# Gate and up of an encoder layer: a second block product by quarter blocks, both in four chained parts

## The chip, the cores and the metric

The kernel runs on one core of a Trainium2 chip. The metric is the device time of one execution in microseconds (us); lower is better. Five engines run side by side, each through its own queue in order: PE (TensorE, matrix products into the accumulator banks), DVE (VectorE), ACT (ScalarE), POOL (GpSimd) and SP, which here only issues transfers. They wait for each other through semaphores.

## The reference

One layer of a bidirectional encoder on 1024 tokens of width 1024, in float32. All but its feed-forward part is left out here:

```
mix = concat(retention, windowed attention) @ w_out
h   = layer_norm(ALPHA * x + mix)                       # (1024, 1024)
g   = h @ w_ffn_gate;   up = h @ w_ffn_up               # (1024, 2816) each
ffn = (silu(g) * up) @ w_ffn_down                       # (1024, 1024)
out = layer_norm(ALPHA * h + ffn + sigmoid(h @ w_pg) * (p @ w_pe))
```

## The kernel before

Each float32 operand is held as two parts, a high part in a shorter format and the remainder (`split`: ScalarE copies the high part, L71, then VectorE subtracts it, L72). A product of two such operands is three matmuls (`mm3c`, L783 to L785).

The large products are done by a scheme with seven block products in place of eight. In gate and up the 22 tiles of 128 hidden units are taken in 11 pairs (`Pair`, n = 0 to 10). The left matrix of a pair, once for gate (m = 0) and once for up (m = 1), is 2 by 2 blocks of 128 hidden units by 512 of the width; the right matrix is the transposed h, 2 by 2 blocks of 512 by 512 in `HB` and, for the sums of blocks that the scheme needs, `TT`. `RIGHT[p]` is the right operand of product p, p = 1 to 7. A *unit* is one product for gate or up: `mm`, 12 matmuls of 512 columns. A bank W takes products 1, 6, 7 and 4 one after another; between them ScalarE copies the running sum to s1, u2, u3. Products 5 and 3 share a bank Z, product 2 has X. The output blocks are c11 = s1 + product 2, c22 = u3 + Z after 5, c21 = W after 4, c12 = u2 + Z after 3; then comes silu(gate) * up (`finish`), and from these sums for the down product (`asum`), stored in `ad`. Left operands are prepared ahead (`prep`: sums of blocks on VectorE, then `split`) into eight operand slots; `raw` and `ln` hold the loaded weights.

From pair 2 on (`FROM`), product 2 is itself done by the seven-product scheme, one level down: quarter blocks of 256 by 256 right columns, for gate and up together (they are the two block rows). That makes 42 matmuls of 256 columns where there were 24 of 512. They come in three parts (`FINE`), with a unit of product 6 between them. Their four right operands that are sums are formed once by VectorE (`fine_right`), each behind a given unit of pairs 0 and 1, in one buffer of 512 columns: three (or two) sums and a split. `prep_fine` prepares the left sums, `post_fine` adds the results to c11 piece by piece.

The order on every engine is written by the recording loop at the end: for each unit k its matmuls, its post, then a piece of `fine`, then preparations of later units (`ahead_g`) as long as slots are free, they lie at most nine units ahead, and the planner's costs fit into the next unit's time: 0.62 for a split, 1.24 for two sums, and so on, less the post's cost and `debt`, which a piece of `fine` raises by 2.2. Stores are issued a given number of units later. Then the down stage (lines from L1410 on) multiplies by w_ffn_down with operands loaded from `ad`.

Of the kernel before, what the change touches and what calls it, by code (L numbers as in the profile page):

```python
# [16 lines left out]
P = 128  # L17
# [25 lines left out]
def layer(tc, xT, xn, w_first, w_mt, w_rv, w_out, w_pg, w_pe, pT, w_gu, w_dn,  # L43
# [1117 lines left out]
    sarena = arena8  # L1161
# [3 lines left out]
    FINE = ((1, 6, 5), (7, 2), (4, 3))  # L1165
    FROM = 2
    evs, nev = [], [0]
    oslots = []
    fright, fsum = {}, []

    def pair_tile():
        nev[0] += 1
        return evs[(nev[0] - 1) % len(evs)]
# [7 lines left out]
    def fine_right(R):  # L1181

        x = cst[:, 0:HF].rearrange("p (k c) -> p k c", k=2)

        def blk(i, j, part):
            return R[:, part, 2 * i:2 * i + 2, j * Q:(j + 1) * Q]

        def both(left, right):
            dve.tensor_tensor(x, blk(*left, 0).bitcast(F32), blk(*right, 0).bitcast(F32), ALU.subtract)
            dve.tensor_tensor(x, x, blk(*left, 1).bitcast(F32), ALU.add)  # L1190
            dve.tensor_tensor(x, x, blk(*right, 1).bitcast(F32), ALU.subtract)

        def less(left):
            dve.tensor_tensor(x, blk(*left, 0).bitcast(F32), x, ALU.subtract)
            dve.tensor_tensor(x, x, blk(*left, 1).bitcast(F32), ALU.add)

        for q, (i, j) in {1: (0, 0), 2: (1, 0), 3: (1, 1)}.items():
            fright[q] = blk(i, j, 0), blk(i, j, 1)
        other = a_tile([P, 2, 2, Q], "fine", dt=F32R)
        fright[7] = other[:, 0], other[:, 1]  # L1200
        fright[5] = tuple(ct([P, 2, Q], "sg", 2, F32R) for _ in range(2))
        fright[6] = tuple(ct([P, 2, Q], "p", 2, F32R) for _ in range(2))
        fright[4] = blk(0, 1, 0), blk(0, 1, 1)
        return [lambda: (both((1, 1), (0, 1)), split(x, *fright[7])), lambda: (both((0, 1), (0, 0)), split(x, *fright[5])),
                lambda: (less((1, 1)), split(x, *fright[6])), lambda: (less((1, 0)), split(x, *fright[4]))]
# [3 lines left out]
    class Pair:  # L1209


        def __init__(self, n):
            self.n = n
            self.raw, self.ops, self.bank, self.ev, self.s, self.fine = {}, {}, {}, {}, {}, {}
# [8 lines left out]
        def sums(self, p, m):  # L1223
            a = lambda i, j: self.raw[m, i, j]
            s = self.s.setdefault(m, [sarena[:, 4 * m + k, :] for k in range(4)])
            if p == 6:
                dve.tensor_tensor(s[1], a(1, 0), a(1, 1), ALU.add)
                dve.tensor_tensor(s[0], s[1], a(0, 0), ALU.subtract)  # L1228
            else:
                dve.tensor_tensor(s[2], a(0, 0), a(1, 0), ALU.subtract)  # L1230
                dve.tensor_tensor(s[3], a(0, 1), s[0], ALU.subtract)
# [9 lines left out]
        def prep_fine(self, part):  # L1241

            f = self.fine

            def xy():
                return [self.raw[m, 0, 1] for m in range(2)]
# [24 lines left out]
            return [[(0, 1.1, sums), (1, 0.62, whole), (1, 0.36, lambda: put(6, fsum[1])), (1, 0.36, lambda: put(5, fsum[0]))],  # L1271
                    [(0, 0.36, lambda: put(7, fsum[2], 5))], [(1, 1.1, last)]][part]

        def mm_fine(self, part):

            if part == 0:
                self.fb = [bank(ptags[(3 * self.n + 1) % 4]) for _ in range(2)]
            for q in FINE[part]:
                t, c0 = self.fine[q]
                i, j = {1: (0, 0), 2: (0, 0), 6: (0, 1), 7: (0, 1), 5: (1, 0), 3: (1, 0), 4: (1, 1)}[q]  # L1280
                o = self.fb[i][:, j * Q:(j + 1) * Q]
                hi, lo = fright[q]
# [3 lines left out]
            for q in ((6,), (7, 2), (4,))[part]:  # L1286
                free_op(self.fine[q][0])

        def post_fine(self, part):

            ev = self.ev
            if part == 0:
                ev["c11"] = pair_tile()
            o, v = ev["c11"], ev["s1"]
            (c11, c12), (c21, c22) = ([o[:, m, j * Q:(j + 1) * Q] for j in range(2)] for m in range(2))
            (bx, by), (bz, bw) = ([b[:, j * Q:(j + 1) * Q] for j in range(2)] for b in self.fb)
            low = o[:, 1, :].rearrange("p (j c) -> p j c", j=2)

            def add(out_, x, y):
                dve.tensor_tensor(out_, x, y, ALU.add)  # L1300

            def twice(b):
                return b.unsqueeze(1).to_broadcast([P, 2, Q])

            if part == 0:
                add(c12, v[:, 0, Q:], bx)
                add(low, v[:, 1, :].rearrange("p (j c) -> p j c", j=2), twice(bx))
                add(c12, c12, by)
            elif part == 1:
                add(low, low, twice(by))  # L1310
                add(c22, c22, bz)
                add(c11, v[:, 0, :Q], bx)
            else:
                add(c12, c12, bz)
                add(c21, c21, bw)
                self.finish("c11", 0)
                self.finish("c11", 1)

        def mm(self, p, m):
            g = {1: 0, 6: 0, 7: 0, 4: 0, 2: 1, 5: 2, 3: 2}[p]  # L1320
            first = p in (1, 2, 5)
            if first:
                self.bank[g, m] = bank(ptags[(3 * self.n + g + (2 if g == 1 and self.n == 0 else 0)) % 4])
# [17 lines left out]

        def post(self, p, m, k):
            ev, W, X, Z = self.ev, self.bank.get((0, m)), self.bank.get((1, m)), self.bank.get((2, m))

            def get(name, over=None):
                if m == 0:
                    ev[name] = ev[over] if over else pair_tile()
                return ev[name][:, m, :]

            def add(name, left, right, over=None):  # L1350
                dve.tensor_tensor(get(name, over), ev[left][:, m, :], right, ALU.add)  # L1351
# [3 lines left out]
            wait = 2 if self.n < NP - 1 else 8  # L1355
            if p == 1:
                act.activation(get("s1"), W, AF.Copy)
# [5 lines left out]
            elif p == 7:  # L1363
                act.activation(get("u3"), W, AF.Copy)
                add("c22", "u3", Z, "u3")
                self.finish("c22", m)
            elif p == 4:
                c = get("c21", "s1")
                if m == 0:
                    act.activation(c, W, AF.Silu)  # L1370
                else:
                    dve.tensor_tensor(c, s("c21"), W, ALU.mult)
                    self.asum("c21", a("c21"), a("c11"), ALU.subtract)
                    stores.append((k + wait, lambda: sp.dma_start(ad[self.n, 2, :, 0, :], s("c21"))))
                    self.asum("c11", s("c21"), a("c22"), ALU.subtract)
                    stores.append((k + wait, lambda: sp.dma_start(ad[self.n, 0], ev["c11"])))
                    self.asum("c22", a("c22"), a("c21"), ALU.subtract)
                    stores.append((k + wait, lambda: sp.dma_start(ad[self.n, 3], ev["c22"])))
            elif p == 3:
                add("c12", "u2", Z, "u2")  # L1380
                self.finish("c12", m)
                if m:
                    self.asum("c12", a("c12"), s("c11"), ALU.add)
                    stores.append((k + wait, lambda: sp.dma_start(ad[self.n, 1], ev["c12"])))
# [5 lines left out]
    def g_unit(n, p, m, k):  # L1390
        pr = pairs2[n]

        def sums():
            pr.sums(p, m)
            if n + 1 < NP and p == 5:
                pairs2[n + 1].load(m, (0,))
# [7 lines left out]
        if p == 6:  # L1404
            items.insert(0, (0, 1.24, sums))
        elif p == 5:
            items.append((0, 1.24, sums))
        after = {2: (0.62, 1.24), 7: (0.62, 1.24), 4: (0, 2.5), 3: (0.62, 1.9)}.get(p, (0, 0))[m]
        return items, lambda: pr.mm(p, m), lambda: pr.post(p, m, k), 2.72, after

    def f_unit(n, part):
        pr = pairs2[n]
        return pr.prep_fine(part), lambda: pr.mm_fine(part), lambda: pr.post_fine(part), (2.16, 1.44, 1.44)[part], 1.45

    for n in range(NP):
        for p in (1, 6, 5, 7, 4, 3) if n >= FROM else (1, 2, 6, 5, 7, 4, 3):
            for m in range(2):
                if n >= FROM and p == 6:
                    gunits.append(f_unit(n, m))
                gunits.append(g_unit(n, p, m, len(gunits)))  # L1420
            if n >= FROM and p == 6:
                gunits.append(f_unit(n, 2))
# [331 lines left out]
    with tc.manual_schedule(engines={ET.PE, ET.DVE, ET.Activation, ET.Pool, ET.SP}):  # L1754
# [3 lines left out]
        fine = fine_right(RIGHT[2])  # L1758
        evs.extend(a_tile([P, 2, HF], "ev") for _ in range(7))
        fsum.extend([cst[:, 0:Q], cst[:, Q:2 * Q], cst[:, 2 * Q:3 * Q], ct([P, Q], "fs", 1)])  # L1760
        ahead_g(-1, 4)
        for k in range(NG):
            gunits[k][1]()
            gunits[k][2]()
            if k in (8, 11, 16, 19):
                fine.pop(0)()
                debt[0] += 2.2
# [4 lines left out]
            if j == -6:  # L1772
                arenas_a()
                op_arena(ct([P, 4, 2, HF], "h0a", dt=F32R))
                op_arena(big16((P, 4, 2, HF)))
                op_arena(big16((P, 4, 2, HF)))
                arena("chain", ct([P, 8, HF], "h0b"), 8)
            if j == -4:
                op_arena(big16((P, 4, 2, HF)))
                arena("b", big.tile([P, 8, HF], F32, tag="H", bufs=4, name=nm("H")), 8)  # L1780
            if j >= -6:
                ahead(0, j + 7)
            if j >= -4:
                ahead(1, j + 5)
        arena("chain", ct([P, 8, HF], "h2"), 8)
# [89 lines left out]
```

## Time and profile before

| | |
|---|---|
| median of 3 runs | 1176.09 us (1175.69 to 1176.13) |
| profiled execution | 1176.84 us, span 1175.1 us |
| granted TensorE clock | 0.998 |
| busy: PE, DVE, ACT, POOL | 1164.5, 845.1, 565.1, 119.2 us |
| gate and up | from 540.8 to 956.6 us of the span |
| down stage | from 956.6 us |

A row of the trace gives the start in us, the duration, engine, line and operation, output <- input by the program's names (buffer numbers left out), shapes, a count where equal rows were merged, and in brackets the engine's idle time before it and what released it. The duration of a row is longer than the distance to the next one where rows overlap in the engine.

### The profile page before, as it was taken

To read this page: it belongs to the slowest core of one execution; us is meant where nothing else is said; L and a number is where in the kernel's file an instruction comes from. 1 tells how busy PE (TensorE), PEld (TensorE's weight loads), DVE (VectorE), ACT (ScalarE), POOL (GpSimd) and SP (SyncE) were. 2 spreads that over 40 slices of the span, in tenths; PEclk is the share of its full clock that TensorE was granted. 3 is DMA by queue.
4 is the path that set the end of the run, shared out by engine and by line. 5 is a ranking of instruction groups with operands and counts; after the bars stand their busy time and mean duration, and the time that the engine had idled before them with its cause. 6 is when DMAs were issued, how large, how long until landed. Compare 5 with 4: busy or idle time off the path is not lost.

```text
span 1175.1 us, 17378 instructions
## 1 busy us (share of the span) xinstructions
PE 1164.5 (99%) x6230; PEld 973.8 (83%) x6230; DVE 845.1 (72%) x1571; ACT 565.1 (48%) x1133; POOL 119.2 (10%) x181
## 2 busy tenths in 40 slices
PE   9999999999999999999999999999999999999996
PEld 7888888888888888888888888888888888888885
DVE  4566678766859688948787777777777766764677
ACT  5566347776756256214344333433434345552463
POOL 2001020202010021000000000000000020224242
PEclk9999999999999999999999999999999999999999
DMA  7345656546346955756232223232232389999977
GB/s 253 103 149 213 242 189 229 200 133 224 110 158 231 377 171 188 269 194 204 96 129 96 101 102 126 76 135 86 113 115 92 110 219 363 339 226 216 262 165 206
DMA packets 80662, 211.73 MB, mean 180 GB/s; under 512 B 9536, under 2 KB 14784, under 8 KB 80576
## 3 DMA queue, kind: packets, MB, share of 16 engines
q1 hardware_dynamic: 71936, 193.84, 46.8%
q0 software_dynamic: 8640, 16.78, 8.2%
q8 instruction: 49, 0.80, 0.3%
q14 instruction: 37, 0.30, 0.1%
HBM read 139.29 MB, written 62.13 MB: 171 GB/s over the span
## 4 chain that ended last, share of the span: by engine, by line
PE 97%; DVE 2%; ACT 1%; issue 0%; DVEq 0%; POOL 0%; POOLq 0%
PE bmm L77 6%; PE bt L783 6%; PE bt L784 6%; PE bt L785 6%; PE bmm L79 6%; PE bmm L78 6%; PE bmm L784 6%; PE bmm L783 6%; PE bmm L785 5%; PE bs L784 5%; PE bs L783 5%; PE bs L785 5%; PE bo L784 5%; PE bo L783 5%; PE bo L785 5%; PE bo L565 2%
## 5 line engine op out<-in xcount | busy, mean ns | idle before, releaser
L77 PE MATMUL bmm<-H,w 128*128 128x512 f32 x240 | 97.5, 406 | 0.0
L79 PE MATMUL bmm<-H,w 128*128 128x512 f32 x240 | 94.1, 392 | 0.0
L78 PE MATMUL bmm<-H,w 128*128 128x512 f32 x240 | 94.0, 392 | 0.0
L1488 POOL DMA_DIRECT2D h0b<-in_w_dn x24 | 21.6, 902 | 538.8 <-DVE h0a L72 507.7
L1334 ACT ACTIVATE ev<-ev 128x512 f32<-128x512 f32 x33 | 20.9, 632 | 74.5 <-DVE ev L1351 63.8
L77 PEld LDWEIGHTS bmm<-H,w 128*128 128x128 f32 x240 | 45.2, 188 | 9.8 <-ACT H L71 0.7
L79 PEld LDWEIGHTS bmm<-H,w 128*128 128x128 f32 x240 | 45.0, 188 | 10.0
L72 DVE TENSOR_TENSOR u<-H,u 128x512 fp32r<-128x512 f32 x47 | 32.1, 689 | 27.9 <-ACT u L71 27.8
L78 PEld LDWEIGHTS bmm<-H,w 128*128 128x128 f32 x240 | 45.2, 188 | 7.9
L72 DVE TENSOR_TENSOR w<-raw,w 128x512 fp32r<-128x512 f32 x50 | 34.2, 691 | 20.9 <-ACT w L71 20.7
L535 ACT ACTIVATE sc<-sc,st 128x385 f32<-128x385 f32 (+1 forms) x64 | 37.2, 585 | 17.0 <-DVE st L533 16.9
L531 DVE CUSTOM_DVE_ANT_0 sc<-cst,bs,skb 128x384 f32<-128x384 f32 (+1 forms) x64 | 34.9, 575 | 9.0 <-PE bs L530 7.7
L72 DVE TENSOR_TENSOR w<-H,w 128x512 fp32r<-128x512 f32 x44 | 30.3, 689 | 15.2 <-ACT w L71 14.6
L71 ACT ACTIVATE w<-raw 128x512 fp32r<-128x512 f32 x50 | 30.7, 623 | 17.4 <-PE bmm L79 6.9
L72 DVE TENSOR_TENSOR u<-raw,u 128x512 fp32r<-128x512 f32 (+1 forms) x32 | 19.7, 616 | 23.5 <-ACT u L71 23.5
L71 ACT ACTIVATE u<-H 128x512 fp32r<-128x512 f32 x47 | 28.9, 622 | 12.4 <-DMA H<-in_w_dn 7.1
L541 ACT ACTIVATE sc<-sc,st 128x384 f32<-128x384 f32 (+1 forms) x64 | 34.1, 581 | 0.8 <-DVE st L539 0.8
L71 ACT ACTIVATE H<-ln 128x512 fp32r<-128x512 f32 (+1 forms) x34 | 22.9, 677 | 23.9 <-DVE ln L1032 7.2
L526 POOL COPY sc<-skb 128x1 f32<-128x1 f32 x64 | 14.7, 237 | 181.7 <-PE bt L553 161.4
L71 ACT ACTIVATE w<-H 128x512 fp32r<-128x512 f32 x44 | 27.4, 622 | 8.4 <-DVE H L1228 8.4
L72 DVE TENSOR_TENSOR H<-ln,H 128x512 fp32r<-128x512 f32 (+1 forms) x34 | 25.0, 747 | 8.1 <-ACT H L71 8.1
L1340 DVE TENSOR_TENSOR ev<-ev,ev 128x512 f32<-128x512 f32 x44 | 29.5, 690 | 1.1
(932 smaller groups left out, 3785.2 us busy)
## 6 DMA issues: line engine op xcount, KB each, us to landing
ad<-ev SPq DMA_DIRECT2D x33, 512.0 KB, 2.6
pgd<-pro SPq DMA_DIRECT2D x28, 512.0 KB, 2.9
raw<-in_w_gu SPq DMA_DIRECT2D x22, 512.0 KB, 3.5
ln<-in_w_gu SPq DMA_DIRECT2D x22, 512.0 KB, 4.1
raw<-ad SPq DMA_DIRECT2D x40, 256.0 KB, 5.7
ln<-ad SPq DMA_DIRECT2D x37, 256.0 KB, 6.5
H<-in_w_dn SPq DMA_DIRECT2D x33, 256.0 KB, 6.4
wod<-aq SPq DMA_DIRECT2D x15, 512.0 KB, 2.7
```

Source lines behind the costliest of these rows:

```text
L71: act.activation(hi, raw, AF.Copy)
L72: dve.tensor_tensor(lo, raw, hi.bitcast(F32), ALU.subtract)
L77: pe.matmul(o, lh, rh, start=start, stop=False)
L78: pe.matmul(o, lh, rl, start=False, stop=False)
L79: recent[0] = pe.matmul(o, ll, rh, start=False, stop=stop).ins.name
L531: dve.tensor_tensor_reduce(sc[g][:, :nk], cst[:, tc0:tc0 + nk], b[:, :nk], slope(i, g), skb[:, 2 * i + g:2 * i + g + 1], ALU.add, ALU.max, ...
L535: act.activation(sc[g][:, :nk + 1], sc[g][:, :nk + 1], AF.Exp, bias=st_[:, 1, j, g:g + 1], accum_out=st_[:, 2, j, g:g + 1])
L541: behind(act.activation(sc[g][:, :nk], sc[g][:, :nk], AF.Copy, scale=st_[:, 3, j, g:g + 1]))
L783: pe.matmul(o, lh, rh, start=start, stop=False, skip_group_check=True)
L784: pe.matmul(o, lh, rl, start=False, stop=False, skip_group_check=True)
L785: pe.matmul(o, ll, rh, start=False, stop=stop, skip_group_check=True)
L1340: dve.tensor_tensor(self.ev[dst][:, 0, :], left, right, op)
```

## The change

Product 4 too is done by quarter blocks, from pair 3 on (`FROM = {2: 2, 4: 3}`). Both such products now come in four parts: quarter products 1, 5, 2; then 6; then 7; then 4, 3. Quarter products 1, 6, 7 and 4 are chained in the left half of one bank, 2 has its right half, and 5 and 3 share the left half of the other bank. Behind each part `post_fine` reads the running sum, always 128 by 256: seven adds a product.

The order of units in a pair changes to `plan`: 1, 1, a part of 2, 6, part, 6, part, 7, part, 7, and then a part of 4, 5, part, 5, part, 3, part, 3. So 7 comes ahead of 5, and the second half of the sums with it. Product 4 by quarters takes its left operands from the loaded up-and-gate blocks directly, and its output block c21 is u3 + the chain. Banks belong to a product now (`TAGS`) and no longer rotate over the pairs; the seven rotating result tiles are six with fixed roles (`homes`); the sums live in two tiles (`sums2`) and partly in the loaded block. The four sums of RIGHT[4]'s quarter blocks are formed as well. All eight pieces of `fine` work in halves of 256 columns through one small buffer, and stand behind units 5, 8, 14, 18, 21, 24, 27 and 42, booked at 2.6. The stage's end books its buffers for the down stage a little later.

```diff
-    FINE = ((1, 6, 5), (7, 2), (4, 3))
-    FROM = 2
+    FINE = ((1, 5, 2), (6,), (7,), (4, 3))
+    FROM = {2: 2, 4: 3}
...
+    TAGS = {0: "t", 1: "o", 2: "mm", 4: "s"}
...
+        f = frights[p] = {q: (blk(*ij, 0), blk(*ij, 1)) for q, ij in {1: (0, 0), 2: (1, 0), 3: (1, 1)}.items()}
+        f.update(zip((7, 5, 6), places))
+        f[4] = blk(0, 1, 0), blk(0, 1, 1)
+        def make(q, left, right):
+            x = fsum[3]
+            for kt in range(2):
+                (lh, ll), (rh, rl) = ([v[:, kt, :].bitcast(F32) for v in side] for side in (left, right))
+                dve.tensor_tensor(x, lh, rh, ALU.subtract)
+                dve.tensor_tensor(x, x, ll, ALU.add)
+                dve.tensor_tensor(x, x, rl, ALU.subtract)
+                split(x, *(v[:, kt, :] for v in f[q]))
+        b = lambda i, j: (blk(i, j, 0), blk(i, j, 1))
+        return [lambda: make(7, b(1, 1), b(0, 1)), lambda: make(5, b(0, 1), b(0, 0)),
+                lambda: make(6, b(1, 1), f[5]), lambda: make(4, b(1, 0), f[6])]
...
+            return [[(0, 1.1, sums), (1, 0.62, whole), (1, 0.36, lambda: put(5, fsum[0]))],
+                    [(1, 0.36, lambda: put(6, fsum[1]))],
+                    [(0, 0.36, lambda: put(7, fsum[2], 6))], [(1, 1.1, last)]][part]
...
-                i, j = {1: (0, 0), 2: (0, 0), 6: (0, 1), 7: (0, 1), 5: (1, 0), 3: (1, 0), 4: (1, 1)}[q]
+                i, j = {1: (0, 0), 6: (0, 0), 7: (0, 0), 4: (0, 0), 2: (0, 1), 5: (1, 0), 3: (1, 0)}[q]
...
+            o, v = (ev["c11"], ev["s1"]) if p == 2 else (ev["c21"], ev["u3"])
+            (ba, bb), bz = [self.fb[p][0][:, j * Q:(j + 1) * Q] for j in range(2)], self.fb[p][1][:, :Q]
+            for out_, x, b in (((c11, v11, ba), (c11, c11, bb)), ((c12, v12, ba),), ((c22, v22, ba), (c22, c22, bz)),
+                               ((c21, v21, ba), (c12, c12, bz)))[part]:
+                dve.tensor_tensor(out_, x, b, ALU.add)
...
+        f = [(2, None, j) for j in range(4)]
+        head = [(1, 0), (1, 1), f[0], (6, 0), f[1], (6, 1), f[2], (7, 0), f[3], (7, 1)]
+        if n < FROM[4]:
+            return head + two(5) + two(4) + two(3)
+        f = [(4, None, j) for j in range(4)]
+        return head + [f[0], (5, 0), f[1], (5, 1), f[2], (3, 0), f[3], (3, 1)]
...
-            if k in (8, 11, 16, 19):
+            if k in (5, 8, 14, 18, 21, 24, 27) or k == FINE4:
                 fine.pop(0)()
-                debt[0] += 2.2
+                debt[0] += 2.6
```

The order on VectorE between the end of pair 1 and the first part of pair 2's product 2; before (L1340 is the last sum of pair 1, L1227 and L1228 the sums for 6 (up), L1267 to the next L72 preparations of the third part, L1300 the post):

```order
L1340 TENSOR_TENSOR ev_5336<-ev_5336,ev_5335 128x512
L1227 TENSOR_TENSOR H_4542<-ln_5707 128x512
L1228 TENSOR_TENSOR H_4542<-H_4542,raw_5682 128x512
L72 TENSOR_TENSOR w_5319<-H_4542,w_5319 128x512
L1267 TENSOR_TENSOR fs_5337<-raw_5641,cst 128x256
L72 TENSOR_TENSOR u_5320<-raw_5682,u_5320 128x256
L72 TENSOR_TENSOR u_5320<-fs_5337,u_5320 128x256
L72 TENSOR_TENSOR w_5321<-H_4542,w_5321 128x512
L1300 TENSOR_TENSOR ev_5332<-ev_5331,bo_5906 128x256
```

and with the change (the second half of a `make`, L1197 to L1199 and the L72 that writes p; then a put, the sums and split for 6 (up), and the post of part 1, L1304):

```order
L1197 TENSOR_TENSOR fs_5338<-h_4932,sg_5328 128x256
L1198 TENSOR_TENSOR fs_5338<-fs_5338,h_4932 128x256
L1199 TENSOR_TENSOR fs_5338<-fs_5338,sg_5329 128x256
L72 TENSOR_TENSOR p_5331<-fs_5338,p_5330 128x256
L72 TENSOR_TENSOR u_5318<-cst,u_5318 128x256
L1227 TENSOR_TENSOR sums_5326<-ln_5747 128x512
L1228 TENSOR_TENSOR sums_5326<-sums_5326,raw_5682 128x512
L72 TENSOR_TENSOR w_5319<-sums_5326,w_5319 128x512
L1304 TENSOR_TENSOR ev_5333<-ev_5335,bo_5950 128x256
L1304 TENSOR_TENSOR ev_5333<-ev_5333,bo_5950 128x256
```

A make of the new kind now stands directly ahead of pair 2's preparations, and the post reads the bank twice.

On ScalarE, at the same place, before (L1334 is the Silu of c12, L1357 the copies of product 1 for gate and up):

```order
L1334 ACTIVATE ev_5336<-ev_5336 128x512
L71 ACTIVATE u_5318<-H_4542 128x512
L71 ACTIVATE w_5317<-cst 128x256
L1357 ACTIVATE ev_5331<-bmm_5866 128x512
L71 ACTIVATE w_5319<-H_4542 128x512
L1357 ACTIVATE ev_5331<-bmm_5884 128x512
```

and with the change (L1324 and L1360 are these lines' new numbers; p is written by the make):

```order
L1324 ACTIVATE ev_5336<-ev_5336 128x512
L71 ACTIVATE w_5317<-sums_5325 128x512
L71 ACTIVATE p_5330<-fs_5338 128x256 x2
L1360 ACTIVATE ev_5335<-bmm_5915 128x512
L71 ACTIVATE u_5318<-cst 128x256
L1360 ACTIVATE ev_5335<-bmm_5931 128x512
```

The copies of product 1 stand behind both splits of the last make now.

More of the change, by code (lines that the diff above doesn't have):

```diff
@@ L1239, in prep, with prep_fine @@
             split(src, t[:, 0, :], t[:, 1, :])
-        def prep_fine(self, part):
-            f = self.fine
+        def prep_fine(self, p, part):
+            f = self.fine[p]
             def xy():
-                return [self.raw[m, 0, 1] for m in range(2)]
+                return [self.raw[m, p == 4, 1] for m in range(2)]
             def sums():
```

179 lines of the change are left out of this document (83 added, 96 removed).

## The prediction

> **What bounds the kernel now.** I read the page first, then the busy time by stage, then the instructions of TensorE and VectorE in order of time. The page:
>
> ```profile
> span 1175.1 us, 17378 instructions
> PE 1164.5 (99%) x6230; PEld 973.8 (83%) x6230; DVE 845.1 (72%) x1571; ACT 565.1 (48%) x1133; POOL 119.2 (10%) x181
> PE 97%; DVE 2%; ACT 1%; issue 0%; DVEq 0%; POOL 0%; POOLq 0%
> ```
>
> TensorE is busy all the span and carries 97% of the chain that ended last. By stretches (us from the span's start; length, then busy time and instructions of PE, PEld, DVE, ACT, POOL, granted clock, DMA share, GB/s): the second pair, which has no quarter blocks, a later pair, and the start of the down stage.
>
> ```profile
> 578.70:616.90 38.20, 38.20 (x170) 31.66 (x169) 30.85 (x51) 16.20 (x30) 0.00 (x0) 1.00 0.37 124
> 654.60:692.30 37.70, 37.70 (x188) 32.03 (x187) 28.07 (x51) 14.60 (x28) 0.00 (x0) 1.00 0.30 105
> 956.00:1000.00 44.00, 44.00 (x196) 36.44 (x195) 29.27 (x47) 25.12 (x45) 6.60 (x8) 1.00 1.03 327
> ```
>
> In gate and up PE has no gap, at full clock. VectorE has 28.07 of 37.70 us, 9.6 us spare a pair. So every us of PE work removed counts, and every us by which VectorE comes too late costs.
>
> **What the change saves on TensorE.** Its matmuls (start, duration, both us): the first of the stage, of pair 2 (the third) and of pair 2's first part of quarter blocks, the end of that part, and the first part of pair 3.
>
> ```profile
> 540.77 0.39 PE L783 MATMUL bt<-h0a,w 128*128 128x512 f32 x1
> 616.93 0.39 PE L783 MATMUL bmm<-h0a,w 128*128 128x512 f32 x1
> 622.37 0.28 PE L783 MATMUL bo<-h0b,w 128*128 128x256 f32 x1
> 624.40 0.28 PE L785 MATMUL bo<-sg,w 128*128 128x256 f32 x1
> 624.52 0.40 PE L783 MATMUL bmm<-H,u 128*128 128x512 f32 x1
> 624.76 0.40 PE L784 MATMUL bmm<-H,u 128*128 128x512 f32 x1
> 660.11 0.28 PE L783 MATMUL bmm<-h0b,u 128*128 128x256 f32 x1
> ```
>
> A unit of 12 matmuls of 512 columns takes (622.37 - 616.93) / 2 = 2.72 us, 0.227 a matmul. The first part's 18 matmuls of 256 columns take 624.52 - 622.37 = 2.15 us, 0.1194 each. A product by quarter blocks needs 42 of these, 5.02 us, in place of 24 x 0.227 = 5.45: 0.43 us less. But the pairs show less: two plain ones take 616.93 - 540.77 = 76.16 us, 38.08 each, and one with quarter blocks 660.11 - 622.37 = 37.74. That is 0.34 saved, so each of the three parts costs 0.03 beside its matmuls; 624.52 to 624.76 (0.24 where 0.227 is usual) is a piece of that. With four parts a product saves 0.43 - 4 x 0.03 = 0.31. Product 4 gets it in eight pairs, 2.5 us, and product 2 pays for a fourth part in nine, 0.3: **-2.2 us**; bounds 8 x 0.43 = -3.4, and -1.5 if a part costs twice as much.
>
> The Trainium skill (TensorE: Matmul & The Clock Gate, section Back-to-back issue gap) gives N / 2.4 + 2.5 ns for a warm matmul of N columns; by it, as an estimate, a product would save 24 x 215.8 - 42 x 109.2 = 593 ns and eight of them 4.7 us. The rows, 227 and 119 ns, disagree, and they decide.
>
> **What it costs on VectorE, first the right operands.** RIGHT[4]'s quarter sums are new, and all eight of them (`make`) are formed in halves of 256 columns, through one buffer. The old `make`, with what comes behind it, and the 256-column rows (three sums; ScalarE's split into the high part):
>
> ```profile
> 566.69 0.68 DVE L1189 TENSOR_TENSOR cst<-h0b 128x512 f32<-128x512 f32 x1
> 567.41 0.69 DVE L1190 TENSOR_TENSOR cst<-cst,h0b 128x512 f32<-128x512 f32 x1
> 568.13 0.69 DVE L1191 TENSOR_TENSOR cst<-cst,h0b 128x512 f32<-128x512 f32 x1
> 568.86 0.63 ACT L71 ACTIVATE fine<-cst 128x512 fp32r<-128x512 f32 x1 [1.42 <-DVE cst L1191]
> 569.53 0.69 DVE L72 TENSOR_TENSOR fine<-cst,fine 128x512 fp32r<-128x512 f32 x1 [0.70 <-ACT fine L71]
> 570.13 0.68 DVE L1351 TENSOR_TENSOR ev<-ev,bmm 128x512 f32<-128x512 f32 x1
> 639.65 0.42 DVE L1250 TENSOR_TENSOR cst<-raw 128x256 f32<-128x256 f32 x1
> 640.10 0.42 DVE L1251 TENSOR_TENSOR cst<-cst,raw 128x256 f32<-128x256 f32 x1
> 640.44 0.42 DVE L1252 TENSOR_TENSOR cst<-raw,raw 128x256 f32<-128x256 f32 x1
> 644.49 0.41 ACT L71 ACTIVATE u<-cst 128x256 fp32r<-128x256 f32 x1
> ```
>
> A 256-column row that needs the one ahead starts 0.45 us behind it, another 0.34; at 512 columns 0.72 and 0.60. The old `make` took 570.13 - 566.69 = 3.44 us. A half of the new one: three dependent sums (0, 0.45, 0.90, done at 1.32), ScalarE's split to 1.76, the subtraction at 1.79; the next half writes the buffer that it reads, so it starts at 2.24, other work at 2.13. Together 4.37 us, 8 x 4.37 = 35 against 4 x 3.44 = 13.8 or less (two of the old ones have a sum less). The planner books 2.6 for each.
>
> Five of the eight stand in pair 1 (behind units 14, 18, 21, 24, 27): 22 us on an engine with some 8 us spare there. What lies ahead of PE's needs must cover the rest. I follow it from the one place where VectorE surely waits for PE, the post of product 5 (gate) in pair 0, nine units after the stage's start: 9 x 2.72 + 0.2 = 24.7 us. From there the order puts 109 rows ahead of what releases part 2 of product 2 in pair 2 (the put of 6 and both reads of part 1): six makes, 54 rows of 512 columns, 7 of 256. Rows that price these, and two waits that come with them (a sum, split by ScalarE, then subtracted; an add whose Silu stands ahead of the next split on ScalarE):
>
> ```profile
> 572.66 0.69 DVE L1227 TENSOR_TENSOR H<-ln 128x512 f32<-128x512 f32 x1
> 573.38 0.69 DVE L1228 TENSOR_TENSOR H<-H,raw 128x512 f32<-128x512 f32 x1
> 574.83 0.69 DVE L72 TENSOR_TENSOR w<-H,w 128x512 fp32r<-128x512 f32 x1 [0.76 <-ACT w L71]
> 575.44 0.68 DVE L1372 TENSOR_TENSOR ev<-ev,bt 128x512 f32<-128x512 f32 x1
> 576.16 2.02 DVE L1340 TENSOR_TENSOR ev<-ev,ev 128x512 f32<-128x512 f32 x3
> 578.10 0.68 DVE L1189 TENSOR_TENSOR cst<-h0b 128x512 f32<-128x512 f32 x1
> 642.62 0.63 ACT L1334 ACTIVATE ev<-ev 128x512 f32<-128x512 f32 x1 [0.75 <-DVE ev L1351]
> 643.81 0.69 DVE L72 TENSOR_TENSOR u<-raw,u 128x512 fp32r<-128x512 f32 x1 [1.22 <-ACT u L71]
> ```
>
> 54 x 0.64 (a third of them dependent) = 34.6; six makes 26.2; 7 small rows 2.7; four splits behind sums 4 x 0.73 = 2.9; one Silu 1.2. Sum 67.6, so part 2 can start at 24.7 + 67.6 = 92.3. TensorE would be there after 30 units of 2.72, part 1 (2.15) and one more unit, 86.5. **+5.8 us**, which nothing returns, since PE has no idle time later to make up. ScalarE says the same: the copy of product 1 that 6 (gate) must wait for stands behind the last make's splits. Bounds: with none of the waits on ScalarE (12 halves x 0.5, 2.9 and 1.2 us) the sum is 57.5 and there is no stall (0); with each row at its whole duration it is 71, a stall of 9. I take the row-by-row value, since the waits of 0.70, 0.76 and 1.22 are measured in the same places.
>
> The Trainium skill (VectorE: DVE Perf Modes, section The DRAIN you can't avoid) says that the next instruction does not start until the pipe has emptied. It speaks against narrow rows; as an estimate it adds 54 x 0.05 + 19 x 0.05 = 3.7 us to the stall. The trace disagrees: 0.42-us rows start 0.34 apart.
>
> The eighth make (behind unit 42, product 3 (gate) of pair 2) delays the first parts of pair 3. VectorE is level with PE at that post, and by the same prices has 13.3 us of rows from there to both reads of part 1 (post 0.6, make 4.4, product 3 (up) 2.05, two puts 0.7, sums and splits of 6 (up) and 7 (gate) 4.7, reads 0.9). PE needs 3 x 2.72 + 2.15 + 2.72 - 0.2 = 12.8. **+0.5**, bounds 0 and 1.
>
> **What it costs in each later pair.** VectorE's rows in a pair of before are 35 of 512 columns and 15 of 256; 35 x 0.64 + 15 x 0.37 = 28.0, which is the 28.07 of the table. With the change there are 32 and 32: 32.3 of 37.3 us. The 5.0 us left hold the waits on ScalarE, and those add to 4 or 5. The tightest piece is from the last part of product 4 to part 2 of the next pair's product 2. After that part's end: drain and wait 0.19, two small adds, Silu, product, three sums 4.17, three rows of 3 (up) 2.05, sums and split of 6 (gate) 2.78, a put 0.36, sums and split of 6 (up) 2.78, the two reads 0.87: 13.2 us. PE gets there in 2.72 x 4 + 2.15 = 13.0. So 0.2 us late a pair, seven pairs **+1.4**; bounds -0.3 (hidden) and +1 each, from the count of waits. The same walk leaves 0.0 to 0.5 us at the other chained parts (product 2's parts 3 and 4, product 4's part 2).
>
> That each part waits for both reads of part 1, though it adds to one half of the bank only, is in the order. The Trainium skill (PSUM — Partial Sum Buffer, section Terms) has two engines on one bank and quadrant at once as an error, so such a wait would be needed there even between halves; no run here shows it. With a wait for the first read alone the 0.2 would be nothing, and the total 1.4 less.
>
> What I cost at nothing: ScalarE's rows (14.6 of 37.7 busy); the loads of the next pair, which are asked for 10 us or more ahead of their use, at a DMA share of 0.30; the stores at two units behind; the down stage, whose first operands are split while VectorE has no next pair to prepare. If that cover is gone, the first product of the down stage comes a unit late, 2.7 us.
>
> **Sum**, on the profiled execution, 1176.84 us with a span of 1175.1: -2.2 + 5.8 + 0.5 + 1.4 = +5.5, 1182.3. The median of the runs shown is 1176.09, 0.75 lower: **1181.6 us**.
>
> **Rivals.** First, **the lead covers the makes**: PE is never held in pair 1 or 2, because the splits on ScalarE run closer behind VectorE's sums than in the rows above, or VectorE enters pair 1 further ahead. It needs 6 us of the 67.6 to vanish. For it: no wait at all is 57.5 us. Against it: each wait is a measured one, and VectorE's floor at 24.7 us is PE's own time. The time is 1176.1 - 2.2 = 1173.9, with the late pairs' 1.4 up to 1175.3. It decides against my forecast as soon as the sum falls under 61.8 us. Second, **VectorE becomes the bound of every pair**: the waits in a pair are 6 us and not 4 to 5, so that a pair takes 38.3 and not 37.3. For it: VectorE now idles 37.70 - 28.07 = 9.6 us a pair. Against it: part of that is VectorE waiting for PE through ScalarE, which goes when VectorE is late. Seven pairs by 1 us: 1181.6 - 1.4 + 7 = 1187.2.
>
> That the change doesn't do what it says is not open: the order has 714 matmuls of 256 columns in this stage where 378 were.
>
> **How the numbers follow.** Forecast 0.70, first rival 0.17, second 0.13. No difference within 0.2% (2.35 us) is what a measurement of this kernel can't tell from nothing. Of the forecast, 0.06 lies within it (a stall of 3 to 4 us); of the first rival 0.12 is faster by more, 0.05 within. So faster 0.12, same 0.11, slower 0.77. The range runs from 1175.0, with most of the first rival below it, to 1187.5, which takes in the second.
>
> **What would show it.** Right: TensorE's only large gaps of the stage in pair 2 at 6 (gate) and at part 2, 5 to 7 us together, perhaps 2 us of it already at 7 (up) of pair 1, released by ScalarE's copies and VectorE's adds behind the makes; makes of 4.3 to 4.5 us; later pairs of 37.3 to 37.6 us. Wrong: no gap before pair 3; or a gap in each later pair near 1 us; or a stall where the down stage begins.

## The result and the profile after

The changed kernel takes 1188.45 us (median of 5 runs, 1187.61 to 1188.74); the kernel before, on the same chip, 1176.13 (1175.69 to 1176.89). The ratio is 1.0103, interval 1.0088 to 1.0118: 12.3 us slower. The forecast was 1181.6 and the range ended at 1187.5: right in sign, and less than half of the size. The page of the changed kernel:

```profile
span 1187.0 us, 17890 instructions
PE 1167.6 (98%) x6374; PEld 981.0 (83%) x6374; DVE 894.8 (75%) x1732; ACT 578.6 (49%) x1177; POOL 119.3 (10%) x181
PE 83%; DVE 9%; ACT 4%; issue 2%; DMA 1%; SPq 0%; DVEq 0%; POOL 0%; ACTq 0%; POOLq 0%
```

VectorE, which carried 2% of the chain that ended last, now carries 9%, and ScalarE 4%. The busy time by stretches (columns as in the prediction): pair 1, pair 2 from its first part on, a later pair, and two short stretches inside the first two.

```profile
578.00:616.00 38.00, 33.30 (x133) 26.69 (x132) 30.45 (x58) 14.30 (x28) 0.00 (x0) 0.91 0.29 104
630.30:672.40 42.10, 39.74 (x187) 32.95 (x187) 34.51 (x68) 17.18 (x34) 0.00 (x0) 0.96 0.27 94
748.30:785.70 37.40, 37.40 (x205) 32.56 (x205) 32.28 (x64) 15.79 (x34) 0.00 (x0) 1.00 0.29 106
602.90:608.60 5.70, 5.70 (x14) 4.50 (x15) 4.38 (x8) 3.20 (x7) 0.00 (x0) 0.50 0.50 184
635.00:639.50 4.50, 4.49 (x13) 3.09 (x13) 3.38 (x7) 1.72 (x5) 0.00 (x0) 0.64 0.00 0
```

TensorE is short of work in pairs 1 and 2, and in each its clock falls for some microseconds (0.50, 0.64). The later pair has no gap. TensorE's rows at each gap (start, duration, in brackets the idle time and what ended it), with the first matmuls of the stage, of product 2's first part in pairs 2, 4 and 10, and of the down stage:

```profile
539.96 0.39 PE L783 MATMUL bmm<-h0a,w 128*128 128x512 f32 x1
...
596.67 0.51 PE L783 MATMUL bmm<-H,w 128*128 128x512 f32 x1 [1.55 <-ACT ev L1362]
599.33 0.39 PE L785 MATMUL bmm<-H,w 128*128 128x512 f32 x1
602.87 0.80 PE L783 MATMUL bmm<-H,u 128*128 128x512 f32 x1 [3.15 <-ACT ev L1362]
...
630.34 0.28 PE L783 MATMUL bo<-h0b,w 128*128 128x256 f32 x1
635.01 0.50 PE L783 MATMUL bmm<-H,w 128*128 128x512 f32 x1 [2.36 <-ACT ev L1360]
639.43 0.49 PE L783 MATMUL bo<-H,u 128*128 128x256 f32 x1
...
677.17 0.39 PE L785 MATMUL bmm<-H,w 128*128 128x512 f32 x1
678.28 0.36 PE L783 MATMUL bo<-H,w 128*128 128x256 f32 x1 [0.71 <-DVE ev L1304]
710.89 0.28 PE L783 MATMUL bo<-h0b,w 128*128 128x256 f32 x1
935.56 0.28 PE L783 MATMUL bo<-h0b,w 128*128 128x256 f32 x1
967.33 0.39 PE L785 MATMUL bt<-h,u 128*128 128x512 f32 x1
968.40 0.47 PE L783 MATMUL bs<-h0a 128*128 128x512 f32 x1 [0.68 <-DVE ev L1304]
```

The same start of the down stage in the trace of before:

```profile
956.59 0.39 PE L783 MATMUL bs<-h0a 128*128 128x512 f32 x1
```

Gate and up grew from 956.59 - 540.77 = 415.82 us to 968.40 - 539.96 = 428.44, by 12.6. From the stage's start to the first part of pair 2 it is 90.38 us in place of 81.60 (+8.8, all in pair 1: gaps at 7 (gate) and 7 (up), then a slow clock). From that part to part 2 it is 9.09 in place of 2.15 + 2.72 (+4.2, at 6 (gate) and at part 2). Pair 3's part 2 is 0.9 late, the down stage begins 0.8 late. These are 14.7 us, 2.1 more than the stage grew by; this remainder is what TensorE saves. A later pair takes (935.56 - 710.89) / 6 = 37.44 us, where it took 37.74.

ScalarE's rows at the second gap of pair 1, and VectorE's of the same time:

```profile
599.63 0.42 ACT L71 ACTIVATE h0b<-fs 128x256 fp32r<-128x256 f32 x1 [3.02 <-DVE fs L1199]
601.92 0.42 ACT L71 ACTIVATE h0b<-fs 128x256 fp32r<-128x256 f32 x1 [1.87 <-DVE fs L1199]
602.24 0.58 ACT L1362 ACTIVATE ev<-bmm 128x512 f32<-128x512 f32 x1
...
608.40 0.60 ACT L1367 ACTIVATE ev<-bmm 128x512 f32<-128x512 f32 x1 [2.50 <-PE bmm L785]
```

```profile
568.15 0.68 DVE L1353 TENSOR_TENSOR ev<-ev,bt 128x512 f32<-128x512 f32 x1
...
598.26 0.42 DVE L1197 TENSOR_TENSOR fs<-h0b,H 128x256 f32<-128x256 f32 x1
600.08 0.43 DVE L72 TENSOR_TENSOR h0b<-fs,h0b 128x256 fp32r<-128x256 f32 x1 [0.48 <-ACT h0b L71]
600.54 0.42 DVE L1197 TENSOR_TENSOR fs<-h0b,H 128x256 f32<-128x256 f32 x1
602.37 0.43 DVE L72 TENSOR_TENSOR h0b<-fs,h0b 128x256 fp32r<-128x256 f32 x1 [0.48 <-ACT h0b L71]
603.37 0.69 DVE L72 TENSOR_TENSOR w<-ln,w 128x512 fp32r<-128x512 f32 x1 [0.58 <-ACT w L71]
...
609.33 0.43 DVE L72 TENSOR_TENSOR H<-fs,H 128x256 fp32r<-128x256 f32 x1 [1.46 <-ACT H L71]
...
638.42 0.87 DVE L1304 TENSOR_TENSOR ev<-ev,bo 128x256 f32<-128x256 f32 x2
```

The make behind unit 18 runs from 598.26 to 602.80. Its two splits on ScalarE wait for its sums (3.02 and 1.87 us), and the copy of 6 (up), on top of which TensorE adds 7 (up), stands behind them in ScalarE's queue. TensorE goes on 0.05 us after that copy's end. So VectorE's lateness reaches TensorE through ScalarE. A little comes back the same way: the copy at 608.40 waits 2.50 us for TensorE, which runs at the slow clock then, the split behind it is late, and VectorE waits 1.46 us at 609.33 where the other halves of a make wait 0.48.

### The profile page after: what moved, and what is told of

It reads as the page before. It is cut to its first block, busy times and chain, and to the rows that moved or that the text cites. A ratio compares the mean times of both kernels' runs of the same rounds, so it can differ in the third digit from the quotient of the medians.

```text
span 1187.0 us, 17890 instructions
## 1 busy us (share of the span) xinstructions
PE 1167.6 (98%) x6374; PEld 981.0 (83%) x6374; DVE 894.8 (75%) x1732; ACT 578.6 (49%) x1177; POOL 119.3 (10%) x181
## 4 chain that ended last, share of the span: by engine, by line
PE 83%; DVE 9%; ACT 4%; issue 2%; DMA 1%; SPq 0%; DVEq 0%; POOL 0%; ACTq 0%; POOLq 0%
PE bmm L783 7%; PE bmm L784 7%; PE bmm L785 7%; PE bmm L77 5%; PE bmm L79 5%; PE bmm L78 5%; PE bt L783 5%; PE bt L784 5%; PE bt L785 5%; PE bs L783 4%; PE bs L785 4%; PE bs L784 4%; PE bo L783 3%; PE bo L785 3%; PE bo L784 3%
## 5 line engine op out<-in xcount | busy, mean ns | idle before, releaser
L77 PE MATMUL bmm<-H,w 128*128 128x512 f32 x240 | 97.4, 406 | 0.0
L79 PE MATMUL bmm<-H,w 128*128 128x512 f32 x240 | 94.2, 393 | 0.0
L78 PE MATMUL bmm<-H,w 128*128 128x512 f32 x240 | 94.1, 392 | 0.0
L1324 ACT ACTIVATE ev<-ev 128x512 f32<-128x512 f32 x41 | 25.9, 633 | 89.8 <-DVE ev L1353 71.4
L72 DVE TENSOR_TENSOR w<-raw,w 128x512 fp32r<-128x512 f32 (+1 forms) x61 | 39.6, 658 | 18.9 <-ACT w L71 18.7
L71 ACT ACTIVATE w<-raw 128x512 fp32r<-128x512 f32 (+1 forms) x61 | 35.8, 597 | 17.4 <-PE bo L79 7.6
L783 PE MATMUL bmm<-H,u 128*128 128x512 f32 x88 | 35.8, 407 | 3.4 <-ACT ev L1362 3.4
L783 PE MATMUL bmm<-H,w 128*128 128x512 f32 x88 | 35.2, 400 | 3.9 <-ACT ev L1360 2.4
L1326 DVE TENSOR_TENSOR ev<-ev 128x512 f32<-128x512 f32 x41 | 28.4, 692 | 12.8 <-ACT ev L1324 11.9
L784 PE MATMUL bmm<-H,u 128*128 128x512 f32 x88 | 35.5, 403 | 0.0
L785 PE MATMUL bmm<-H,u 128*128 128x512 f32 x88 | 35.3, 401 | 0.0
L1353 DVE TENSOR_TENSOR ev<-ev,bt 128x512 f32<-128x512 f32 x44 | 30.0, 682 | 6.7 <-PE bt L785 6.7
L784 PE MATMUL bmm<-H,w 128*128 128x512 f32 x88 | 35.0, 398 | 0.0
L785 PE MATMUL bmm<-H,w 128*128 128x512 f32 x88 | 35.0, 398 | 0.0
L71 ACT ACTIVATE H<-ln 128x512 fp32r<-128x512 f32 (+1 forms) x34 | 22.9, 677 | 21.5 <-DVE ln L1032 7.2
```

What stands on the lines that cost most here:

```text
L71: act.activation(hi, raw, AF.Copy)
L72: dve.tensor_tensor(lo, raw, hi.bitcast(F32), ALU.subtract)
L77: pe.matmul(o, lh, rh, start=start, stop=False)
L78: pe.matmul(o, lh, rl, start=False, stop=False)
L79: recent[0] = pe.matmul(o, ll, rh, start=False, stop=stop).ins.name
L783: pe.matmul(o, lh, rh, start=start, stop=False, skip_group_check=True)
```

## The experiments

Theory A: VectorE has too many rows of the makes between the stage's start and part 2 of pair 2. Theory B: the parts themselves cost. Theory C: the halved clock costs by itself. Later came two on order: D, only the planner's order is wrong, and Q, a place in ScalarE's queue decides. Each ratio is to runs of the kernel before on the same chip, whose medians were 1176.28, 1176.88 and 1176.95 us in the three sets of four; what a version costs over the kernel before is taken against its own set (the changed kernel: +12.3).

**The makes without their sums.** In each half of a make:

```
-                dve.tensor_tensor(x, lh, rh, ALU.subtract)
-                dve.tensor_tensor(x, x, ll, ALU.add)
-                dve.tensor_tensor(x, x, rl, ALU.subtract)
-                split(x, *(v[:, kt, :] for v in f[q]))
+                split(lh, *(v[:, kt, :] for v in f[q]))
```

> The eight right operands of the quarter blocks are only split (ScalarE's copy and one subtraction on VectorE for each half): the three sums of each half are left out. TensorE's instructions, the parts, their order and all other waits stay those of the changed kernel. Theory A (the stall is VectorE's: too many rows of the makes between the stage's start and part 2 of product 2 in pair 2): six makes lose 6 x 2 x 1.35 = 16 us of that chain, more than the 13 us of stall, so the stall goes and the PE saving of 2.2 stays: 1174 to 1176 us. Theory B (the parts themselves cost: chained banks, reads between parts, the new order of the posts): the time stays at 1184 to 1188.

Measured: 1175.56 us, ratio 0.9992 (0.9983 to 1.0001). TensorE's first matmul of this stage and the first of the down stage:

```profile
540.98 0.39 PE L783 MATMUL bmm<-h0a,w 128*128 128x512 f32 x1
...
955.59 0.47 PE L783 MATMUL bs<-h0a 128*128 128x512 f32 x1 [0.66 <-DVE ev L1301]
```

The stage takes 414.6 us with the same parts, banks and posts, 13.8 less. Theory B falls: without the sums none of the stalls ahead of the down stage is left. With the 0.8 that is lost ahead of the down stage here too, the saving on TensorE is 415.8 - 414.6 + 0.8 = 2.0 us, about the forecast's value. VectorE's post of 5 (gate) in pair 0, which stands at 568.15 in the changed kernel, waits for TensorE here, 24.9 us into the stage:

```profile
565.87 0.69 DVE L1350 TENSOR_TENSOR ev<-ev,bt 128x512 f32<-128x512 f32 x1 [0.88 <-PE bt L785]
```

**Product 2 only, four makes.** FROM[4] is set past the last pair, and makes stand only behind units 5, 8, 14 and 18.

> Product 4 stays a plain product in all pairs and its four makes are left out; product 2 is by quarter blocks in four parts from the third pair on, with its four makes at the first four places (behind units 5, 8, 14 and 18). Theory A: three makes less stand ahead of part 2 of pair 2, 13.5 us of VectorE, so no stall; the fourth part costs 0.3 against the kernel before: 1176 to 1177.3 us. Theory B (four parts chained in one bank cost by themselves): over 1179.

Measured: 1184.0, 1.0065 (1.005 to 1.008), so the expectation missed. It counted VectorE up to pair 2 alone. Pair 2 has no stall, but pair 1 has both of its gaps (1.4 us ahead of 7 (gate), 3.2 ahead of 7 (up)), since all makes ahead of them are the same four. The second:

```profile
603.39 0.50 PE L783 MATMUL bmm<-H,u 128*128 128x512 f32 x1 [3.19 <-ACT ev L1362]
```

Product 2 alone, with its makes in their new form and places, costs 7.7 us.

**All eight makes, product 4 plain.**

```
-    FROM = {2: 2, 4: 3}
+    FROM = {2: 2, 4: 99}
...
-                split(x, *(v[:, kt, :] for v in f[q]))
+                split(x, *(v[:, kt, :] for v in f[7 if p == q == 4 else q]))
```

> Product 4 stays plain in all pairs, but all eight makes are formed at the places of the change (product 4's four results are used by nothing, the last of them written over the first). Theory A: the stall of pairs 1 and 2 is all there, and the saving of product 4's quarter blocks (eight pairs of 0.30) and pair 3's 0.9 are not: 1188.5 + 2.4 - 0.9 = 1190 us (1188.5 to 1191). Theory B (product 4 by quarters is what costs): 1176 to 1178.

Measured: 1189.98, 1.0113 (1.0098 to 1.0128), as theory A has it. Product 4's quarter blocks are not what costs; its makes are: this run is 13.7 us over the kernel before, the one with product 2's four makes alone 7.7, so product 4's four cost 6.0.

**TensorE kept busy in the gaps.** Extra matmuls into an idle bank:

```
+            fill = {(1, 7, 0): 7, (1, 7, 1): 14, (2, 6, 0): 20}.get((self.n, p, m), 0)
+            if fill:
+                spare = bank("s")
+            for _ in range(fill):
+                pe.matmul(spare, RIGHT[1][:, 0, 0, 0:P], RIGHT[1][:, 0, 0, :], start=True, stop=True, skip_group_check=True)
```

> The changed kernel with extra matmuls of 512 columns into a bank that nothing uses then, put where TensorE idles: 7 ahead of 7 (gate) and 14 ahead of 7 (up) in pair 1, 20 ahead of 6 (gate) in pair 2. TensorE then has no idle time there and should keep its full clock at 602.9 to 608.6 us, where it had 0.50. Theory A (VectorE's chain sets when part 2 begins; the half clock lies beside it, but for about 1 us in which ScalarE's copy waited for TensorE): 1187 to 1189 us. Theory C (the half clock is a loss of its own): 5.7 us at half rate and 2.4 us at 0.64 come back, 1184 to 1185.

Measured: 1187.81, 1.0097 (1.008 to 1.0113). The clock from 602.9 to 608.6 us is 1.00 where it was 0.50, and 0.999 over the whole profiled execution where it was 0.994. The time over the kernel before goes from 12.3 to 11.5 us, not to 8. Up to the first part of pair 2, 3.0 us are back (87.37 us from the stage's start for 90.38), but only 1.1 up to part 2 (98.36 for 99.47), which still waits for VectorE's reads (1.37 us). Of the 1.1, 1.0 is what came back through ScalarE: the half of a make that waited 1.46 us waits 0.48 here. So in the changed kernel nearly all of the slow clock lies beside VectorE's chain.

**The sums on GpSimd.** `pool.tensor_tensor` for the 24 sums, whole, from unit 2 on, into a tile of the pair that is idle then; whole splits 2 to 5 units behind them.

> The changed kernel with the 24 sums of the eight right operands formed on GpSimd, whole (512 columns), early and into a tile of the pair that is idle then; ScalarE and VectorE split each, whole, some units later. VectorE keeps 8 rows of 512 columns of the makes' 64 of 256. GpSimd has nothing else to do in this stage; its rows of 128 and 256 columns took 0.50 and 0.68 us elsewhere, so by these some 1.0 us for one of 512. Theory A (VectorE's rows of the makes cause the stall): no stall, the 2.25 us saved on TensorE that the run without sums showed in this stage, 0.9 lost where the down stage begins: 1174.3 to 1176. Rival: the two engines hinder each other, VectorE's 512-column rows get longer than 0.68 us while GpSimd works and the stall of pair 1 stays in part: over 1178.

Measured: 1188.36, 1.009 (1.0077 to 1.0103): nothing gained, and the rival is right; GpSimd's rows took 1.3 to 1.7 us and not the 1.0 estimated. Of one stretch, first GpSimd's rows (POOL), then VectorE's:

```profile
571.22 1.63 POOL L1196 TENSOR_TENSOR ev<-ev,h0b 128x512 f32<-128x512 f32 x1
...
577.71 1.62 POOL L1197 TENSOR_TENSOR ev<-ev,h 128x512 f32<-128x512 f32 x1
```

```profile
571.62 0.67 DVE L1356 TENSOR_TENSOR ev<-ev,bt 128x512 f32<-128x512 f32 x1
...
578.10 1.77 DVE L1230 TENSOR_TENSOR sums<-ln 128x512 f32<-128x512 f32 x1
579.91 0.69 DVE L1231 TENSOR_TENSOR sums<-sums,raw 128x512 f32<-128x512 f32 x1
```

While GpSimd works, VectorE's rows of 0.69 us with both operands in SBUF take up to 1.78. The row at 571.62, one of whose operands is a bank, keeps 0.67 although GpSimd is at work on a sum then. So a sum taken off VectorE gives its time to the rows beside it.

**Whole makes.** The three sums and the split on 512 columns, at the change's places:

```
-            for kt in range(2):
-                (lh, ll), (rh, rl) = ([v[:, kt, :].bitcast(F32) for v in side] for side in (left, right))
+            (lh, ll), (rh, rl) = ([v.bitcast(F32) for v in side] for side in (left, right))
```

with x a buffer of 512 columns that is idle then.

> The changed kernel with its eight makes at the same places, but each formed whole (three sums and a subtraction of 512 columns, as the kernel before had them) and not in two halves of 256. A make should then take 3.5 us in place of 4.5. Theory A: the six makes between the post of 5 (gate) of pair 0 and part 2 of product 2 in pair 2 give back 6 us, the two before them 1 or 2: 1181 to 1184. Rival (width doesn't matter, since the waits for ScalarE and not the rows set a make's length): 1187 to 1189.

Measured: 1180.5, 1.0027 (1.0017 to 1.0038): 3.6 us over the kernel before where halves cost 12.3, so 8.7 less, more than expected. The make behind unit 18:

```profile
595.45 0.69 DVE L1197 TENSOR_TENSOR cst<-h0b,H 128x512 f32<-128x512 f32 x1
596.17 0.69 DVE L1198 TENSOR_TENSOR cst<-cst,h0b 128x512 f32<-128x512 f32 x1
596.90 0.69 DVE L1199 TENSOR_TENSOR cst<-cst,H 128x512 f32<-128x512 f32 x1
598.29 0.69 DVE L72 TENSOR_TENSOR h0b<-cst,h0b 128x512 fp32r<-128x512 f32 x1 [0.70 <-ACT h0b L71]
```

598.98 - 595.45 = 3.53 us, where two halves took 4.54 (598.26 to 602.80). One us on each of eight makes is 8. Only 0.26 us of the one comes from waiting for ScalarE (twice 0.48 against 0.70). The other 0.75 is rows: half the columns are not half the time. From one dependent row to the next it is 0.46 us at 256 columns and 0.72 at 512, so a make's eight narrow rows take 3.58 us and its four wide ones 2.83. Halves through two buffers, where the second half's sums could fill the first half's wait, were not tried.

**Whole and spread.** Makes as in the run above; product 4 by quarter blocks a pair later, and

```
-    FROM = {2: 2, 4: 3}
+    FROM = {2: 2, 4: 4}
...
-            if k in (5, 8, 14, 18, 21, 24, 27) or k == FINE4:
+            if k in (8, 11, 16, 19, 30, 37, 46) or k == FINE4:
```

where FINE4 is then unit 58.

> Whole makes as in the run above, and spread: product 2's behind units 8, 11, 16 and 19, as in the kernel before, product 4's behind units 30, 37, 46 and 58, and product 4 by quarter blocks from the fifth pair on (seven pairs and not eight). Theory A: VectorE never falls behind by more than its lead, no stall but perhaps 1 us at the pairs with a make; 2.25 - 0.3 saved, 0.9 lost at the down stage: 1175 to 1177. If it stays over 1180, the makes are not what holds TensorE in pair 1.

Measured: 1176.13, 0.9992 (0.9983 to 1.0001). TensorE has no gap in the stage but the one where the down stage begins.

**The planner books 3.6 us for a make, not 2.6.**

> The changed kernel with one number changed: the planner books 3.6 us and not 2.6 for each make, so that it puts less preparation of later units between the makes and the posts that follow them. No row is added or taken away. Theory A (too many rows in too little time): the chain to part 2 of pair 2 holds nearly the same rows; at most the preparations of units 33 to 36, 5 us, move behind it: 1183 to 1188. Theory D (there is time enough, and only the order is wrong: preparations that are needed 10 us later stand ahead of copies for which TensorE waits): 1175 to 1178.

Measured: 1192.09, 1.0127 (1.0112 to 1.0142), worse than either theory said. TensorE's waits from pair 1 to pair 3 in this run, on the bank of products 1, 6, 7 and 4 (in total, times, longest):

```profile
PE bmm L783 <- ACT ev L1362: 4.7, 2, 2.9
PE bmm L783 <- ACT w L71: 4.5, 2, 4.0
PE bmm L783 <- ACT u L71: 1.7, 1, 1.7
```

The copies of product 6 (L1362) are as late as in the changed kernel, and 6.2 us of waits for operands (L71) are new. The longest, 4.0, stands at 6 (gate) of pair 2, where the changed kernel waited 2.4 for the copy of product 1. What the planner put off was then missing: the preparations ahead of the posts were needed. Theory D falls in this form.

**Whole, spread, and other banks at the down stage.** Its first products start in banks that were read long before:

```
-    dsets = (("s", "t"), ("o", "mm"))
+    dsets = (("o", "t"), ("s", "mm"))
```

> Whole and spread makes as before, and the two banks that the first products of the down stage take are swapped with two that have long been read by then. What is left between the stages should go: 0.9 us, so 1175.2 (1174.7 to 1175.9), under the kernel before by 0.9. Rival (the wait is for ScalarE's and VectorE's splits of that product's operands, and the bank is only what the trace names): 1176.

Measured: 1175.21, 0.9987 (0.9978 to 0.9996). The last matmul of gate and up and the first of the down stage:

```profile
954.16 0.39 PE L785 MATMUL bt<-h,u 128*128 128x512 f32 x1
954.38 0.39 PE L783 MATMUL bo<-h0a 128*128 128x512 f32 x1
```

The gap is gone (0.22), and the version is ahead of both kernels, of the one before by 0.13%, which its interval just clears.

**Product 2 only, gaps filled.** The second run with 7 and 14 extra matmuls in pair 1.

> Only product 2 by quarter blocks, as in the second run, with 7 extra matmuls ahead of 7 (gate) and 14 ahead of 7 (up) of pair 1. Here no later wait hides the half clock that followed the gap of 3.3 us (604.2 to 607.5 us, 7 matmuls 0.427 apart in place of 0.227, and two or three slower ones). Theory C: 1.6 us come back, 1182.4. Theory A says the same of this kernel only if VectorE waits for TensorE right after; if VectorE is still behind there, 1184 as without the extra matmuls.

Measured: 1182.8, 1.0048 (1.0035 to 1.0062): 5.9 us over the kernel before in place of 7.7, so 1.8 back. The two intervals overlap, but the traces agree: from the first matmul of 7 (up) to the first of 5 (gate) it is 2.85 us in place of 4.45, 1.6 less, and the clock from 604.0 to 607.6 us is 1.00 in place of 0.55. Where no later wait hides it, the slow clock is a loss of its own.

**Product 2 only, the fourth make behind unit 19.**

> Only product 2 by quarter blocks, as in the second run, with the fourth make behind unit 19, product 6 (up) of pair 1, and not behind unit 18. The same rows; ScalarE's copy of 6 (up), for which TensorE waited 3.3 us, then stands ahead of that make's two splits and not behind them. Theory Q (the place in ScalarE's queue decides: the splits wait for VectorE's sums and the copy waits with them): that gap goes and the half clock with it, 1184.0 - 3.3 - 1.6 = 1179. Theory A in its simple form (only the number of rows counts): 1184, the stall moves to the next copy.

Measured: 1179.29, 1.002 (1.0011 to 1.0029): 2.3 us over the kernel before in place of 7.7, so 5.4 back with the same rows, as theory Q has it. On VectorE the make also changes places with three preparations of later units, which now stand ahead of it; on ScalarE the copy of 6 (up) stands ahead of the make's splits. 7 (up) follows 7 (gate) without a gap:

```profile
600.00 0.39 PE L785 MATMUL bmm<-H,w 128*128 128x512 f32 x1
600.22 0.39 PE L783 MATMUL bmm<-H,u 128*128 128x512 f32 x1
```

**Halves, spread.** The change's makes at the places of the whole and spread run.

> The changed kernel's makes in halves at the spread places (8, 11, 16, 19; 30, 37, 46, 58; product 4 by quarter blocks from the fifth pair on): the fourth corner beside halves at the change's places (1188.4), whole at the change's places (1180.5) and whole and spread (1176.1). If the places decide: 1176 to 1178. If each make's extra us is not covered in pairs 0 and 1 either: 4 us more up to pair 1, so 1179 to 1181.

Measured: 1183.08, 1.0054 (1.004 to 1.0068), more than either side expected. The expectation had looked at pairs 0 and 1; most of the loss is at chained parts in pairs 2 to 4, where product 4's makes stand now and TensorE waits for VectorE's posts (in total, times, longest; 590 to 720 us):

```profile
PE bo L783 <- DVE ev L1304: 4.0, 4, 1.1
PE bmm L783 <- ACT ev L1362: 0.9, 2, 0.6
```

Over the kernel before, the four corners are +12.3 (halves, the change's places), +6.1 (halves, spread), +3.6 (whole, the change's places) and -0.8 (whole, spread). So halves cost 8.7 and 6.9 us, the places 6.2 and 4.4, each good to some 2 us by the intervals. The spread ones count seven pairs and not eight, 0.3 us.

## Why the prediction was right in sign and wrong in size

- **TensorE's saving, -2.2.** Right: 2.1 as the remainder of the stretches above, 2.0 from the run without sums. The estimate of 4.7 that the prediction worked out from the Trainium skill (TensorE: Matmul & The Clock Gate, section Back-to-back issue gap) does not agree with these. The bound of -1.5 left out product 2's own fourth part at the doubled price (9 x 0.06); with it, it is -1.0.
- **The stall up to part 2 of pair 2, +5.8.** The mechanism was right, and the run without sums shows it: VectorE's makes, felt through ScalarE's copies. The size failed: 99.47 us from the stage's start where 86.5 was free, +13.0, over the bound of 9. The step that failed is the sum 24.7 + 67.6. Its start was named as a place where VectorE surely waits for TensorE. The row at 568.15 has no wait and stands 28.2 us into the stage, not 24.7: VectorE was 3.5 us late there already. The first make, behind unit 5, stands ahead of that row, and the prediction took it for covered. In the run without sums, with the same splits of later units ahead of it, the row waits for TensorE and stands at 24.9, with 0.88 us to spare; so the lead there is one of 0.88 us, and the first make's sums use it up. The chain's length was 71.1 us (568.15 to 639.29), not 67.6. The rows are the ones it counted. VectorE waited 1.9 us for ScalarE in places that the sum did not have (0.58, 0.36, and the 1.46 above where 0.48 is usual). The six makes took 0.08 us more each than the 4.37, without that 1.46, 0.5 in all; the rest is spread over the other rows.
- **Where it shows.** Pair 2 at 6 (gate) and part 2 was right, and so were the releasers; "perhaps 2 us of it already at 7 (up)" was far too little: 8.8 of the 13.0 fall into pair 1. The prediction had the place in ScalarE's queue for pair 2 only; in pair 1 the same thing happens behind unit 18, and moving that one make by a unit gave 5.4 us back in the kernel with product 2 alone.
- **Pair 3, +0.5.** 0.9, within its bounds.
- **Later pairs, +1.4.** Wrong: they run without a stall at 37.44 us, within the 37.3 to 37.6 given. By the prediction's own saving a pair without a stall is 38.08 - 2 x 0.31 = 37.46, so nothing is left for the 0.2 us a pair. In one of them the piece from the last part of product 4 to both reads of part 1 took 12.8 us (777.59 to 790.39) and not 13.2, and TensorE needed 13.1. The second rival, VectorE as the bound of every pair, is refuted.
- **The down stage, nothing.** Wrong by 0.8: the bank, not an operand, was late, since quarter blocks of product 4 now use the bank that the down stage takes first. The swap of banks shows it.
- **The first rival, the lead covers the makes.** It is what whole and spread makes do; at the change's places and in halves the lead is short by 13 us.
- **VectorE's narrow rows.** The sentence that the prediction took from the Trainium skill (VectorE: DVE Perf Modes, section The DRAIN you can't avoid) has an exception in the same section, for an instruction that is not held. So the rows 0.34 us apart need not disagree with it, and the 3.7 us do not follow from it.

The sum by terms: -2.1 + 13.0 + 0.9 + 0 + 0.8 = 12.6 against -2.2 + 5.8 + 0.5 + 1.4 = 5.5. A make was priced within 4%. The miss came half from where VectorE stood when the chain began, behind a make that the sum left out, and half from the chain's length.

## What to carry to other kernels

An engine with a quarter of its time to spare can still hold the busy one for 13 us: what counts is its backlog at the place where the one-off work stands, and a chain's start must be read from a row that waits, not from where it ought to wait. Before a chain of sums on one engine is cut in halves, price the half rows: here a row of half the width took 0.42 us and not half of 0.69, and each half had its own wait for ScalarE, together 1 us a make. And look at what stands behind a late split in the same queue, since a copy there passes the lateness on.

## What was not expected of the hardware

VectorE's rows of 512 columns with both operands in SBUF took 1.77 us in place of 0.69 while GpSimd formed sums there, and a row with an operand in a bank kept 0.67. The Trainium skill (SBUF — State Buffer, section SBUF: two separate sides) has the two engines hold one port pair by turns, VectorE's instructions with two SBUF inputs among them; the rows agree.

TensorE's clock fell to 0.50 for 5.7 us after gaps of 1.6 and 3.2 us close together, and to 0.64 over a stretch that followed a gap of 2.4. A gap of 1.6 alone, in the run with the fourth make behind unit 19, left the matmuls 0.23 us apart. In the run with whole makes they were 0.43 us apart after a gap of 1.9:

```profile
627.60 0.57 PE L783 MATMUL bmm<-H,w 128*128 128x512 f32 x1 [1.88 <-ACT ev L1365]
627.97 0.63 PE L784 MATMUL bmm<-H,w 128*128 128x512 f32 x1
628.40 0.63 PE L785 MATMUL bmm<-H,w 128*128 128x512 f32 x1
```

The Trainium skill (TensorE: Matmul & The Clock Gate, section Part 1: The HAM clock gate) puts the fall to half after about 3.4 us of idling; here shorter gaps were enough.
